# A batched matrix product: VectorE as a loop of four turns, and transfers that wait for VectorE's finished copies

## The chip, the cores and the metric

The kernel runs on one core of a Trainium2 chip. The time is the device time of one execution in microseconds (us); three runs of the kernel before gave 513.1, 514.22 and 514.61, median 514.22. The engines are called PE (TensorE), DVE (VectorE), ACT (ScalarE), POOL (GpSimd) and SP (SyncE). Transfers between HBM and SBUF go through 16 DMA engines; the queue q0 holds those that POOL issues, q1 those that SP issues.

## The reference

```
x:      (32, 512, 1024) float32
weight: (32, 1024, 768) float32
return np.matmul(x, weight).astype(np.float32)
```

Thirty-two independent products, each of a 512 x 1024 matrix with a 1024 x 768 matrix.

## The kernel before

The batches are taken two at a time: 16 pairs, k = 0 to 15, and pair k holds the batches 2k and 2k + 1. Every engine has its own stream of instructions, written out by hand, and the streams meet only at semaphores.

**Loads (POOL).** A load casts float32 from HBM to bfloat16 in SBUF. The weights have four slots, for four batches. Batches 0 to 3 and 30 and 31 are loaded one at a time (L101), those between by pairs in one transfer (L97), which needs the slots of the pair two before. The rows of x have two slots, for two pairs (L110); x of pair 0 comes by SP in float32 and is cast by DVE and ACT (L279). POOL issues in a fixed order: the first five loads at once, then for each k from 0 to 13 x of pair k + 2, from k = 2 on the store of pair k - 2 (L118), and the weights of pair k + 2. It stops at each wait, so a late wait also holds back what is written behind it. All these transfers share q0.

**What the loads wait for.** Weights wait for `s_mm`, which PE raises at the end of each half set of matmuls, four times a batch: when it has reached `mm_done(b)`, all matmuls of batch b are done. x waits for `s_pt`, which PE raises after each of the eight groups of transposes of a pair: the x of pair k - 2 is then read.

**Transposes and products (PE).** PE is a loop over the pairs. It takes `s_xr` (x has landed), transposes x in eight groups g into two PSUM tiles `pt` (L173), takes `s_wr` for each batch (the weights have landed, L177), and multiplies: for each batch four row tiles mt, each of 8 x 2 matmuls, one of 512 columns (L165) and one of 256 (L138). Two row tiles make a set p, so a batch has two sets, and a set fills three PSUM banks. The number of an output set is j = 2b + p.

**Copies (DVE and ACT).** DVE copies each group of transposes to SBUF (`spread`, L226, in the last pair L224). Of each set, DVE copies the bank shared by the two row tiles (L269, two copies, which raise `s_d`) and half of the third bank (L271, which raises `s_dp`); ACT copies the first bank (L258, `s_a`) and the other half of the third (L261, `s_ap`). PE waits for `s_c` (spreads), `s_a` and `s_d` before it overwrites a bank. In DVE's straight stream the order for pair k is: eight spreads, the last set of pair k - 1, then the first three sets of pair k. The last set of a pair is thus copied after the spreads of the next pair.

**Stores.** A pair's outputs are stored in one transfer by POOL, two pairs late (`HELD`), once `s_ap` and `s_dp` show them copied; the last pairs go by SP (L118 and L123). There are four slots of outputs; the first set of a pair waits until the slot's last store has landed (`slot_free`), on DVE and on ACT each.

Of the kernel before, what the change touches and what calls it, by code (L numbers as in the profile page):

```python
# [8 lines left out]
BF16 = mybir.dt.bfloat16  # L9
# [3 lines left out]
def kernel(  # L13
# [6 lines left out]
    nc = tc.nc  # L20
    B, M, K = x.shape
# [4 lines left out]
    KT = K // P  # L26
# [3 lines left out]
    PAIRS = B // 2  # L30
    HELD = 2
    GROUPS = 2 * MT
    W_SLOTS, X_SLOTS, OUT_SLOTS = 4, 2, 4

    pe, dve, act, pool, sp = nc.tensor, nc.vector, nc.scalar, nc.gpsimd, nc.sync
# [7 lines left out]
    def sbuf(name, shape, dtype):  # L43
        return nc.alloc_sbuf_tensor(name, shape, dtype).ap()
# [5 lines left out]
    both = [sbuf(f"xT{i}", [P, 2, JT, 2, H, 2], BF16) for i in range(MT)]  # L50
# [3 lines left out]
    pts = [nc.alloc_psum_tensor(f"pt{i}", [P, JT, P], F32).ap() for i in range(2)]  # L54
# [6 lines left out]
    def sem(name):  # L61
        sems.append(nc.alloc_semaphore(name))
        return sems[-1]
# [2 lines left out]
    s_w = [sem(f"s_w{i}") for i in range(W_SLOTS)]  # L66
    s_x = [sem(f"s_x{i}") for i in range(X_SLOTS)]
    s_wr, s_xr = sem("s_wr"), sem("s_xr")
    s_pt, s_c, s_mm = sem("s_pt"), sem("s_c"), sem("s_mm")
    s_a, s_ap, s_d, s_dp = sem("s_a"), sem("s_ap"), sem("s_d"), sem("s_dp")  # L70
    s_st = [sem(f"s_st{i}") for i in range(OUT_SLOTS)]
    s_fin = sem("s_fin")

    def mm_done(b):
        return 4 * (b + 1)

    def pt_done(k):
        return GROUPS * (k + 1)  # L80

    def last_out(b):

# [5 lines left out]
    def together(b):  # L89
        return W_SLOTS <= b < B - 2  # L90

    def load_w(b):
        if together(b):
            if b % 2 == 0:
                pool.wait_ge(s_mm, mm_done(b + 1 - W_SLOTS))
                slots = all_ws[:, b // 2 % 2].rearrange("p r ko n -> p r (ko n)")
                pool.dma_start(out=slots, in_=w_two_view[b // 2]).then_inc(s_w[b % W_SLOTS], 16)  # L97
            return
        if b >= W_SLOTS:
            pool.wait_ge(s_mm, mm_done(b - W_SLOTS))  # L100
        pool.dma_start(out=ws[b % W_SLOTS], in_=w_view[b]).then_inc(s_w[b % W_SLOTS], 16)  # L101

    def loads_of_w(b):
# [2 lines left out]

    def load_x(k):
        if k >= X_SLOTS:
            pool.wait_ge(s_pt, pt_done(k - X_SLOTS))
        pool.dma_start(out=xs[k % X_SLOTS], in_=x_view[k]).then_inc(s_x[k % X_SLOTS], 16)  # L110

    def copied(eng, j):
# [14 lines left out]
    def stationary(b, mt):  # L127
        return both[mt][:, b % 2].rearrange("p j h i r -> p j (h i) r")
# [7 lines left out]
    def other(out, weights, moving, first, last):  # L136

        return pe.add_instruction(  # L138
            mybir.InstMatmult(
                name=nc.get_next_instruction_name(),  # L140
                engine=mybir.EngineType.PE,
                ins=[pe.lower_ap(moving), pe.lower_ap(weights)],
                outs=[pe.lower_ap(out)],
                start_tensor_calc=first,
                stop_tensor_calc=last,
                tile_size=(P, P),
                tile_position=(0, 0),
                ldweights=False,
            )
        )  # L150

    def multiply(b, mt, w):
        pm, half = pms[mt // 2], mt % 2
        xT = stationary(b, mt)
        for ko in range(KT):
            for i, (bank, at, off, size) in enumerate(SPLITS[half]):
                args = (
                    pm[bank][:, at:at + size],
                    xT[:, ko // 2, :, ko % 2],
                    w[:, ko, off:off + size],  # L160
                )
                if i:
                    last = other(*args, ko == 0, ko == KT - 1)
                else:
                    last = pe.matmul(*args, start=(ko == 0), stop=(ko == KT - 1))  # L165
        last.then_inc(s_mm, 1)

    def transpose(k, g):

# [43 lines left out]

    def spread(k, g):

        pt = pts[g % 2].bitcast(BF16).rearrange("p j (b i r) -> p j b i r", b=2, r=2)
        if k == PAIRS - 1:

            for b in range(2):
                rows = both[g // 2][:, b].rearrange("p j h i r -> p j (h i r)")
                rows = rows.rearrange("p j (m r) -> p j m r", r=2)[:, :, g % 2::2, :]
                last = dve.tensor_copy(rows, pt[:, :, b])  # L224
            return last
        return dve.tensor_copy(both[g // 2][:, :, :, g % 2].rearrange("p b j i r -> p j b i r"), pt)  # L226

    def slot_free(eng, a):
        if a >= OUT_SLOTS:
            eng.wait_ge(s_st[a % OUT_SLOTS], 16 * (a // OUT_SLOTS))  # L230

    def columns(two_rows, i):

# [5 lines left out]
    def pieces(b, p, i):  # L239

        pm = pms[p][i]
        if i == 1:
            pm = pm.rearrange("p (t n) -> p t n", t=2)
        rows = [slice(0, H), slice(H, P)]
        at = p * N2
        if b >= B - 2:
            return [(columns(last_out(b)[half, at:at + N2], i), pm[half]) for half in rows]
        mine = outs[(b // 2) % OUT_SLOTS][H * (b % 2):H * (b % 2 + 1)]
        starts = [at + h * ROW for h in range(2)]
        return [(columns(mine[:, at:at + N2], i), pm[half]) for at, half in zip(starts, rows)]  # L250

    def out_on_act(b, p):
        j = 2 * b + p
        if b % 2 == 0 and p == 0:
            slot_free(act, b // 2)
        act.wait_ge(s_mm, 2 * j + 1)
        for piece in pieces(b, p, 0):
            last = act.copy(*piece)  # L258
        last.then_inc(s_a, 1)
        act.wait_ge(s_mm, 2 * j + 2)  # L260
        act.copy(*pieces(b, p, 2)[0]).then_inc(s_ap, 1)  # L261

    def out_on_dve(b, p):
        j = 2 * b + p
        if b % 2 == 0 and p == 0:
            slot_free(dve, b // 2)
        dve.wait_ge(s_mm, 2 * j + 2)
        for piece in pieces(b, p, 1):
            last = dve.tensor_copy(*piece)  # L269
        last.then_inc(s_d, 1)  # L270
        dve.tensor_copy(*pieces(b, p, 2)[1]).then_inc(s_dp, 1)  # L271

    def cast_first(eng, copy, rows):

        eng.wait_ge(s_first, 16)
        for mo in rows:
            if mo == 2 * MT - 1:
                eng.wait_ge(s_cast, 1)
            last = copy(xs[0][:, mo], x_first[:, mo])  # L279
        return last  # L280

    def on_dve():

        dve.sem_inc(s_d, 2)
        cast_first(dve, dve.tensor_copy, range(MT)).then_inc(s_cast, 1)
        for k in range(PAIRS):
            for g in range(GROUPS):
                dve.wait_ge(s_pt, GROUPS * k + g + 1)
                spread(k, g).then_inc(s_c, 1)
            for j in range(4 * k - 1, 4 * k + 3):  # L290
                if j >= 0:
                    out_on_dve(*divmod(j, 2))
        out_on_dve(B - 1, 1)

    def on_act():
        act.sem_inc(s_a, 2)
        cast_first(act, act.copy, range(MT, 2 * MT)).then_inc(s_xr, 1)
        for b in range(B):
            out_on_act(b, 0)
            if b % 2 and b < B - 1:  # L300
                landed(act, s_x[(b // 2 + 1) % X_SLOTS], (b // 2 + 2) // 2, s_xr)
            out_on_act(b, 1)
# [5 lines left out]
    def on_pool():  # L308
        load_w(0)
        pool.memset(ident, 0.0).then_inc(s_zero, 1)  # L310
        pool.wait_ge(s_zero, 1)
        pool.affine_select(  # L312
            out=ident,
            in_=ident,
            compare_op=mybir.AluOpType.not_equal,
            fill=1.0,
            base=0,
            pattern=[[-1, P]],
            channel_multiplier=1,
        ).then_inc(s_ident, 1)  # L320
        load_w(1)
        load_x(1)
        load_w(2)
        load_w(3)
        for k in range(PAIRS - 2):
            load_x(k + 2)
            if k >= 2:
                store(pool, k - 2, s_st[(k - 2) % OUT_SLOTS])
            load_w(2 * k + 4)
            load_w(2 * k + 5)  # L330
        for a in range(PAIRS - 2 - HELD, PAIRS - 2):
            store(pool, a, s_st[a % OUT_SLOTS])
# [21 lines left out]
    with tc.tile_critical(sync_engine=mybir.EngineType.Activation, no_gpsimd_drain=True):  # L354
        sp.dma_start(x_first, x_view[0]).then_inc(s_first, 16)
        on_pool()
        on_pe()
        on_dve()
        on_act()
        on_sp()  # L360
        clear_on_pool()
# [30 lines left out]
```

## Time and profile before

| what | value |
|---|---|
| median of three runs | 514.22 us |
| the profiled execution, its own time | 515.02 us |
| its span, first to last instruction | 512.9 us |
| PE busy | 430.9 us, 84% of the span |
| DVE busy | 212.9 us, 42%, 332 instructions |
| ACT busy | 116.4 us, 23% |
| POOL busy | 29.0 us, 6% |
| granted clock of PE, mean | 0.947 |
| stores on q0, issue to landing, median | 50.8 us |
| weights by pairs, issue to landing, median | 39.6 us |
| x, issue to landing, median | 43.2 us |

Busy times are those of one profiled execution, which ran 0.8 us longer than the median. A PE that is busy is not a PE at its peak, since the ends of matmuls are modelled. Waiting, branch and semaphore instructions don't count as busy. "Issue to landing" runs from the issuing instruction to the semaphore that says that all data is there, so it holds the time in the queue behind earlier transfers.

### The profile page before, as it was taken

To read this page: it belongs to the slowest core of one execution; us is meant where nothing else is said; L and a number is where in the kernel's file an instruction comes from. 1 tells how busy PE (TensorE), PEld (TensorE's weight loads), DVE (VectorE), ACT (ScalarE), POOL (GpSimd) and SP (SyncE) were. 2 spreads that over 40 slices of the span, in tenths; PEclk is the share of its full clock that TensorE was granted. 3 is DMA by queue.
4 is the path that set the end of the run, shared out by engine and by line. 5 is a ranking of instruction groups with operands and counts; after the bars stand their busy time and mean duration, and the time that the engine had idled before them with its cause. 6 is when DMAs were issued, how large, how long until landed. Compare 5 with 4: busy or idle time off the path is not lost. (4 is left out here: it accounts for less than half of the span.)

```text
span 512.9 us, 5613 instructions
## 1 busy us (share of the span) xinstructions
PE 430.9 (84%) x2512; PEld 174.7 (34%) x1536; DVE 212.9 (42%) x332; ACT 116.4 (23%) x197; POOL 29.0 (6%) x54
## 2 busy tenths in 40 slices
PE   0299999999997996969979699896997969989990
PEld 0143435353534242242423424224242332523420
DVE  0243736354545343352433524435353353533731
ACT  1313131313231221302213022130321303223130
POOL 2000001010101000010000100001000010000000
PEclk9999999999999998988989889899998989989996
DMA  8999999999999999999999999999999999999996
GB/s 293 263 212 215 221 222 206 226 293 246 219 338 214 335 222 229 323 219 339 217 245 308 219 336 216 272 287 219 333 218 290 265 220 339 216 299 254 366 427 253
DMA packets 9446, 136.37 MB, mean 266 GB/s; under 512 B 864, under 2 KB 864, under 8 KB 1376
## 3 DMA queue, kind: packets, MB, share of 16 engines
q0 software_dynamic: 8576, 125.83, 95.2%
q1 hardware_dynamic: 864, 10.49, 4.9%
q14 instruction: 6, 0.05, 0.0%
HBM read 167.77 MB, written 50.33 MB: 425 GB/s over the span
## 5 line engine op out<-in xcount | busy, mean ns | idle before, releaser
L165 PE MATMUL pm<-w,xT 128*128 x976 | 337.0, 394 | 0.0
L138 PE MATMUL pm<-w,xT 128*128 x1024 | 287.8, 281 | 36.2 <-PEq L177 29.0
L165 PEld LDWEIGHTS pm<-w,xT 128*128 128x128 bf16 x1024 | 103.4, 101 | 276.6 <-issue 275.9
L269 DVE COPY outs<-pm 64x512 f32<-64x512 f32 x128 | 88.1, 689 | 200.5 <-PE pm L138 199.1
L258 ACT COPY outs<-pm 64x512 f32<-64x512 f32 x128 | 74.2, 580 | 275.5 <-PE pm L138 274.8
L173 PE MATMUL pt<-ident,x 128*128 128x128 f32 x512 | 84.9, 309 | 33.3 <-PEq L177 23.0
L226 DVE COPY xT<-pt 128x1024 bf16<-128x1024 bf16 x120 | 77.7, 687 | 66.0 <-PE pt L173 65.9
L173 PEld LDWEIGHTS pt<-ident,x 128*128 128x128 f32 x512 | 71.6, 210 | 48.6 <-issue 26.4
L261 ACT COPY outs<-pm 64x512 f32<-64x512 f32 x64 | 37.0, 578 | 91.5 <-PE pm L138 91.5
L271 DVE COPY outs<-pm 64x512 f32<-64x512 f32 x64 | 43.9, 686 | 0.0
L97 POOL DMA_DIRECT2D w<-in_weight_dram x13 | 9.2, 704 | 298.6 <-PE pm L138 298.6
L110 POOL DMA_DIRECT2D x<-in_x_dram x15 | 8.3, 554 | 90.0 <-PE pt L173 90.0
L279 DVE CAST x<-outs 128x1024 bf16<-128x1024 f32 x4 | 2.5, 688 | 18.8 <-DMA outs<-in_x_dram 18.8
L118 POOL DMA_DIRECT2D out_dram<-outs x14 | 7.5, 537 | 8.0 <-DVE outs L271 7.7
L279 ACT CAST x<-outs 128x1024 bf16<-128x1024 f32 x4 | 3.9, 1042 | 16.5 <-DMA outs<-in_x_dram 16.5
L224 DVE COPY xT<-pt 128x512 bf16<-128x512 bf16 x16 | 5.7, 417 | 4.2 <-PE pt L173 4.2
L101 POOL DMA_DIRECT2D w<-in_weight_dram x6 | 3.4, 565 | 26.6 <-PE pm L138 25.3
L279 ACT ACT_TABLE_LOAD x1 | 1.3, 1283 | 1.0 <-ACTq L354 1.0
L312 POOL TENSOR_SCALAR_AFFINE_SELECT ident<-ident 128x128 f32<-128x128 f32 x1 | 0.3, 283 | 0.2 <-POOL ident L310 0.2
L310 POOL MEMSET ident<- 128x128 f32 x1 | 0.2, 223 | 0.0
L376 POOL MEMSET const-float32-0.0<- 128x1 f32 x1 | 0.1, 100 | 0.2 <-issue 0.2
L376 POOL MEMSET const-bfloat16-1.0<- 128x1 bf16 x1 | 0.1, 103 | 0.0
(2 smaller groups left out, 0.2 us busy)
## 6 DMA issues: line engine op xcount, KB each, us to landing
out_dram<-outs POOLq DMA_DIRECT2D x14, 3072.0 KB, 50.8
w<-in_weight_dram POOLq DMA_DIRECT2D x13, 3072.0 KB, 39.6
x<-in_x_dram POOLq DMA_DIRECT2D x15, 2048.0 KB, 43.2
w<-in_weight_dram POOLq DMA_DIRECT2D x6, 1536.0 KB, 40.0
outs<-in_x_dram SPq DMA_DIRECT2D x1, 4096.0 KB, 17.8
out_dram<-outs SPq DMA_DIRECT2D x1, 3072.0 KB, 18.4
out_dram<-outs SPq DMA_DIRECT2D x4, 768.0 KB, 12.2
```

Of the source, the lines that this page charges most:

```text
L97: pool.dma_start(out=slots, in_=w_two_view[b // 2]).then_inc(s_w[b % W_SLOTS], 16)
L110: pool.dma_start(out=xs[k % X_SLOTS], in_=x_view[k]).then_inc(s_x[k % X_SLOTS], 16)
L118: eng.dma_start(out=two_view[a], in_=outs[a % OUT_SLOTS]).then_inc(sem, 16)
L138: return pe.add_instruction(mybir.InstMatmult(name=nc.get_next_instruction_name(), engine=mybir.EngineType.PE, ins=[pe.lower_ap(moving), p ...
L165: last = pe.matmul(*args, start=(ko == 0), stop=(ko == KT - 1))
L173: last = pe.transpose(pts[g % 2][:, j, :], words[:, mo, j::JT], ident)
L226: return dve.tensor_copy(both[g // 2][:, :, :, g % 2].rearrange("p b j i r -> p j b i r"), pt)
L258: last = act.copy(*piece)
L261: act.copy(*pieces(b, p, 2)[0]).then_inc(s_ap, 1)
L269: last = dve.tensor_copy(*piece)
L271: dve.tensor_copy(*pieces(b, p, 2)[1]).then_inc(s_dp, 1)
L279: last = copy(xs[0][:, mo], x_first[:, mo])
```

## The change

DVE's stream of 16 pairs becomes a loop of four turns over four pairs. A register `turn` counts the turns; branches leave out the copy of a set before the first pair and choose other copies in the last one. Constants can't tell the turns apart, so the semaphores that DVE waits for are counted down: `s_set` (new) is raised by PE once for each finished set and taken by DVE, `s_free` (new) is raised by ACT when it has seen that a slot is free, and `s_pt` is lowered by 32 at the end of each turn. With `s_pt` and `s_mm` no longer counts over the whole run, the loads wait for `s_dp`, DVE's last copy of a set.

```diff
+    def out_done(b):
+        return 2 * (b + 1)
+
+    def out_before(k):
+        return 4 * k
...
     def load_w(b):
         if together(b):
             if b % 2 == 0:
-                pool.wait_ge(s_mm, mm_done(b + 1 - W_SLOTS))
+                pool.wait_ge(s_dp, out_done(b + 1 - W_SLOTS))
...
         if b >= W_SLOTS:
-            pool.wait_ge(s_mm, mm_done(b - W_SLOTS))
+            pool.wait_ge(s_dp, out_done(b - W_SLOTS))
...
     def load_x(k):
         if k >= X_SLOTS:
-            pool.wait_ge(s_pt, pt_done(k - X_SLOTS))
+            pool.wait_ge(s_dp, max(out_before(k - X_SLOTS), 1))
...
-                    last = pe.matmul(*args, start=(ko == 0), stop=(ko == KT - 1))
-        last.then_inc(s_mm, 1)
+                    full = pe.matmul(*args, start=(ko == 0), stop=(ko == KT - 1))
+        if half:
+            full.then_inc(s_mm, 1)
+        last.then_inc(s_set if half else s_mm, 1)
...
+    def slot_free(a):
         if a >= OUT_SLOTS:
-            eng.wait_ge(s_st[a % OUT_SLOTS], 16 * (a // OUT_SLOTS))
+            act.wait_ge(s_st[a % OUT_SLOTS], 16 * (a // OUT_SLOTS)).then_inc(s_free, 1)
...
+    def set_on_dve(b, p):
+        dve.wait_ge(s_set, 1).then_inc(s_set, -1)
         for piece in pieces(b, p, 1):
             last = dve.tensor_copy(*piece)
         last.then_inc(s_d, 1)
...
+        dve.sem_inc(s_free, OUT_SLOTS)
+        turns = PAIRS // OUT_SLOTS
+        def spreads(k, copy):
             for g in range(GROUPS):
                 dve.wait_ge(s_pt, GROUPS * k + g + 1)
-                spread(k, g).then_inc(s_c, 1)
-            for j in range(4 * k - 1, 4 * k + 3):
-                if j >= 0:
-                    out_on_dve(*divmod(j, 2))
-        out_on_dve(B - 1, 1)
+                copy(g).then_inc(s_c, 1)
+        def sets(b):
+            dve.wait_ge(s_free, 1).then_inc(s_free, -1)
+            set_on_dve(b, 0)
+            set_on_dve(b, 1)
+            set_on_dve(b + 1, 0)
+        with nc.Fori(0, turns, engines=[mybir.EngineType.DVE], hint_back_edge=True):
+            for k in range(OUT_SLOTS - 1):
+                spreads(k, spread)
+                if k:
+                    set_on_dve(2 * k - 1, 1)
+                else:
+                    with dve.If_ne(turn, 0):
+                        set_on_dve(2 * OUT_SLOTS - 1, 1)
+                sets(2 * k)
+            k = OUT_SLOTS - 1
+            with dve.If_ne(turn, turns - 1):
+                spreads(k, spread)
+            with dve.If_eq(turn, turns - 1):
+                spreads(k, spread_last)
+            set_on_dve(2 * k - 1, 1)
+            with dve.If_ne(turn, turns - 1):
+                sets(2 * k)
+            with dve.If_eq(turn, turns - 1):
+                sets(B - 2)
+            step = GROUPS * OUT_SLOTS
+            dve.wait_ge(s_pt, step).then_inc(s_pt, -step)
+            dve.reg_add(turn, turn, 1)
+        set_on_dve(B - 1, 1)
```

In the changed file, L98 and L102 are the weight loads of L97 and L101, L112 the x load of L110, and L274 and L276 the copies of L269 and L271.

## The prediction

> **What bounds the kernel now.** I read the queues first (columns: packets, MB, share of the time of 16 engines).
>
> ```profile
> q0 software_dynamic: 8576, 125.83, 95.2%
> q1 hardware_dynamic: 864, 10.49, 4.9%
> HBM read 167.77 MB, written 50.33 MB: 425 GB/s over the span
> ```
>
> The two queues together fill 100% of the span. PE, the busiest engine, has 84%. Next the stages: one from the time when the pairs take 26.5 us, one from the time when they take 31.5 us (length, then busy us of each engine; DMA share and GB/s last).
>
> ```profile
> 60.00:86.00 26.00, 25.02 (x155) 10.47 (x95) 12.86 (x20) 6.59 (x12) 1.80 (x3) 1.00 1.00 212
> 188.00:219.50 31.50, 26.73 (x159) 10.82 (x97) 13.10 (x20) 6.89 (x13) 1.76 (x3) 0.95 1.02 266
> ```
>
> The DMA share is 1.0 in both, and PE is idle for almost 5 us of the second. What PE waits for is in its waits (total, times, longest):
>
> ```profile
> PE pm L138 <- PEq L177: 29.0, 8, 4.4
> ```
>
> L177 is the wait for weights. It comes in most pairs from 160 us on, never between 30 and 160 us. So PE sets the pace at first, while the transfers queue up; then the queue does. Over the whole run the queue never pauses, so **any time in which it is empty is added to the end**. That decides this case.
>
> How full the queue is when POOL issues is read from POOL's timeline and, for each issue, from the time to landing (last column).
>
> ```profile
> 51.62 0.70 POOL L97 DMA_DIRECT2D w<-in_weight_dram  x1 [20.45 <-PE pm L138]
> 57.30 0.56 POOL L110 DMA_DIRECT2D x<-in_x_dram  x1 [4.97 <-PE pt L173]
> 78.10 0.70 POOL L97 DMA_DIRECT2D w<-in_weight_dram  x1 [20.25 <-PE pm L138]
> 83.78 0.56 POOL L110 DMA_DIRECT2D x<-in_x_dram  x1 [4.97 <-PE pt L173]
> 84.35 0.54 POOL L118 DMA_DIRECT2D out_dram<-outs  x1
> ```
>
> The answers for the windows 30:31 (x of pair 2, issued at 30.63), 51:52, 57:58 and 78:79, in this order:
>
> ```profile
> x<-in_x_dram POOLq DMA_DIRECT2D x1, 2048.0 KB, 31.1
> ```
> ```profile
> w<-in_weight_dram POOLq DMA_DIRECT2D x1, 3072.0 KB, 24.7
> ```
> ```profile
> x<-in_x_dram POOLq DMA_DIRECT2D x1, 2048.0 KB, 29.0
> ```
> ```profile
> w<-in_weight_dram POOLq DMA_DIRECT2D x1, 3072.0 KB, 22.7
> ```
>
> So x(2) lands at 61.7, w(4,5) at 76.3, x(3) at 86.3, w(6,7) at 100.8: one after another, a pair of weights in 14.6 us and an x in 10.0. By the trace's packets the engines go over from x(2) to w(4,5) between 60.8 and 61.5 (middle 61.1), and from x(3) to w(6,7) between 85.0 and 85.9 (middle 85.3). The issues at 51.62 and 78.10 thus come 9.5 and 7.2 us ahead of the queue's end. These are the two thinnest covers of the run. Store 0, issued at 84.35, lands 34.2 us later at 118.5; a store takes 7.2 us (x(4) lands at 111.3). From there a pair costs the queue 14.6 + 10.0 + 7.2 = 31.8 us against PE's 26.5, and the cover grows by some 5 us a pair. At 188 us weights land 40.5 us after their issue: 26 us queued ahead.
>
> **The change part by part.**
>
> *Weights wait for DVE's last copy (s_dp) and no longer for the last matmul (s_mm).* The last copy of a pair stands on DVE behind the eight spreads of the next pair, which wait for PE's transposes. DVE's timeline:
>
> ```profile
> 57.76 1.39 DVE L269 COPY outs<-pm 64x512 f32<-64x512 f32 x2
> 59.08 0.69 DVE L271 COPY outs<-pm 64x512 f32<-64x512 f32 x1
> ...
> 84.24 1.39 DVE L269 COPY outs<-pm 64x512 f32<-64x512 f32 x2
> 85.55 0.69 DVE L271 COPY outs<-pm 64x512 f32<-64x512 f32 x1
> ```
>
> The L271 copies that release w(4,5) and w(6,7) end at 59.08 + 0.69 = 59.8 and at 86.2. The issues move from 51.6 to 59.8 and from 78.1 to 86.3: **8.2 us later**, and the cover of 9.5 and 7.2 becomes 1.3 and -1.0 us.
>
> What this leaves empty depends on the time L from POOL's issue to the first packet, which no issue into an empty queue shows in mid-run. The rows that bound it: the first weight load, at the start of the run, and SP's load of x, issued at 0.93 with its first packet at 1.9 (another queue, L = 1.0).
>
> ```profile
> 1.49 0.67 POOL L101 DMA_DIRECT2D w<-in_weight_dram  x1 [1.04 <-ACTq L354]
> ```
> ```profile
> q0 software_dynamic: 16, 0.20, 92.6%
> ```
>
> The second is the window 6:7; 1:6 has no packet of q0. By the packets the first begins at 6.23, so L = 4.7, of which up to 1.2 may be the wait for a running packet of x (1.22 us each): 3.5 to 4.7. I take 3.5, from the same queue and operation, at its low end since a first use may be slower.
>
> - First hole: 59.8 + 3.5 = 63.3 against 61.1: 2.2 us.
> - Second hole: x(3) then ends at 85.3 + 2.2 = 87.5; w(6,7) begins at 86.3 + 3.5 = 89.8: 2.3 us.
> - Third issue, w(8,9): DVE's copies before it end at 112.9, so it begins by 116.4. Store 0 ends at about 117.3 + 4.5 = 121.8: no hole, nor later.
>
> Sum: 89.8 - 85.3 = **4.5 us**; in general 1.0 + L, so 2.0 (SP's row) to 5.7 us.
>
> The Trainium skill ("DMA: Bandwidth & Descriptors", Specifications) gives a first-byte latency of about 1 us for transfers that GpSimd issues; by it the loss would be estimated at 2.0 us, while the only row of that queue here has 4.7 with the wait named above.
>
> Does PE stop in the early part? w(4,5) lands at about 78.5 and is needed at 83.8; w(6,7) at about 105.3, needed at 110.4. No. The loss returns later: weights land 4.5 us later in every pair from 160 us on, the waits at L177 begin earlier and take the sum up. With 26 us queued ahead, an issue 8.2 us later leaves some 17 there: nothing more is lost per pair.
>
> *x waits for s_dp too.* Its issue moves from 57.3 to about 60.5, behind w in the same queue, as before, and the store after it by the same 3 us. Queue order on POOL is unchanged; w and x now go out in one burst. x(2) waits for the first copy (ends 37.8, was issued at 30.6); w(3) lands only at 52.1. Nothing. At the end, w(31) moves from 443.4 to 451.6, where the last L271 ends; it landed at 482.8 with 32 us ahead of its own 7.3, and PE needs it at about 490. Nothing.
>
> *The loop and branches on DVE.* DVE's instructions in the built program go from 356 to 168; the copies executed are the same. A back edge with branches is shown on PE: L173's idle by "issue" is 26.4 us in 16 pieces, 23.0 of it the first, so 0.23 us for each of the others. Four turns with some six branches each make about 6 us on DVE at that price, but most stand ahead of a spread, where DVE is idle for 3.7 us a pair, or ahead of a copy. The issues of w(4,5) and w(6,7) have no branch since the first turn's start ahead of them. Cost 0; uncovered, up to 0.2 us at the place of each hole.
>
> *s_set, s_free, and the earlier s_mm for half sets.* ACT's third copy may start one 256-wide matmul earlier (0.28 us); DVE is the last at the end, so nothing is gained. ACT reaches the wait for a slot ahead of DVE. Cost 0. Gain, at most those 0.28 us.
>
> **Time.** The profiled execution took 515.0 (span 512.9 and 2.1 around it): 519.5 after. It lies 0.8 above the median of 514.2, so I forecast **518.7** for the median.
>
> **Rivals.**
> - *Quick start of the queue*: L near 1.0 as in SP's row, a loss of 2.0, 516.2. For it: the 4.7 may hold first-use costs. Against: it is the only row of this queue. 0.13.
> - *Not slower: the hole is made up for.* If PE and not the queue sets the end, 4.5 us of hole are caught up and the time stays at 514.2; the point is whether the queue has 4.5 us to spare anywhere after 90 us. For it: the chain of waits of the last 93 us is all PE, and in 508:512 the queue is nearly idle. Against: the share of 1.02 in mid-run; PE's start in pair 14 (451.17) follows the landing of its weights (410.41 + 40.1 = 450.5), so PE's end hangs on the queue. 0.15; with the scatter of 513.1 to 514.6 this holds all chance of faster.
> - *Stalls on DVE*: each back edge or skipped block makes DVE wait for instructions. The instruction queue moves 6 packets in the span now. A stall decides only beyond DVE's 3.7 us of idle time plus the queue's cover, 5 us at the first edge (near 125 us) and 17 later; 10 us there would add about 1.5, to 520 or more. 0.07. The Trainium skill ("Runtime: NRT & Kernel Launch", Instruction fetch mechanics) says that a taken branch to a target outside two blocks of 256 instructions must fetch it first; no run here shows such a stall yet.
> - *The change doesn't do what it says* (issues not later): the waits in the diff leave no room. 0.
>
> **How the numbers follow.** Forecast 0.65 (517 to 520.5 by L and the scatter), the rivals as above. A measurement of this kernel tells 0.3% (1.5 us) from no change. Slower: 0.65 + 0.07 + most of 0.13 = 0.84; same: 0.11; faster: 0.05. The range runs from 514.8, which takes in the quick start, to 522, which takes in L = 4.7 and some of the stalls.
>
> **What would show it.** POOL's L98 issues at about 59.8 and 86.3 with landings of w(4,5) near 78.5 and w(6,7) near 105; a DMA share clearly under 1 near 62 and 88 and nowhere else; waits for weights that begin a pair earlier. The forecast is wrong if the share shows no hole, if holes show elsewhere (in late pairs above all), or if PE waits for DVE.

## The result and the profile after

| | before | changed |
|---|---|---|
| median of 6 runs each | 513.72 us | 517.25 us |
| ratio, 95% interval | | 1.007 (1.0051 to 1.0088) |
| profiled execution, own time | 515.02 us | 517.05 us |
| its span | 512.9 us | 515.3 us |

The changed kernel is slower by 3.5 us, with an interval of 2.6 to 4.5 us (0.51 and 0.88% of 513.7). 518.7 was forecast.

The queues of the changed kernel, in the same view as before:

```profile
q0 software_dynamic: 8576, 125.83, 95.1%
q1 hardware_dynamic: 864, 10.49, 4.9%
HBM read 167.77 MB, written 50.33 MB: 423 GB/s over the span
```

The bytes are the same, and the rate over the span fell from 425 to 423 GB/s. A hole of some 2 us doesn't show in a share of 515. It must be looked for in the stages. First POOL's timeline of the changed kernel, then the landings of the two weight loads in it (windows 59:60.3 and 86:86.8):

```profile
59.88 0.71 POOL L98 DMA_DIRECT2D w<-in_weight_dram  x1 [21.35 <-DVE outs L276]
60.57 0.56 POOL L112 DMA_DIRECT2D x<-in_x_dram  x1
86.36 0.71 POOL L98 DMA_DIRECT2D w<-in_weight_dram  x1 [25.23 <-DVE outs L276]
```
```profile
w<-in_weight_dram POOLq DMA_DIRECT2D x1, 3072.0 KB, 17.6
```
```profile
w<-in_weight_dram POOLq DMA_DIRECT2D x1, 3072.0 KB, 17.3
```

The issues come at 59.9 and 86.4, released by DVE's L276 and no longer by PE. The loads land 17.6 and 17.3 us later, where 24.7 and 22.7 were shown before. A load of this size takes 14.6 us when it follows another, so almost nothing was queued ahead any more. Its weights are there at 77.5 and 103.7, 1.2 and 2.9 us later than before.

Two stretches of 5 us, of the kernel before and of the changed one (length, busy us of PE, PEld, DVE, ACT, POOL, granted clock, DMA share, GB/s):

```profile
61.00:66.00 5.00, 4.95 (x32) 1.52 (x16) 1.98 (x3) 1.73 (x3) 0.00 (x0) 1.00 1.08 229
85.00:90.00 5.00, 5.00 (x33) 1.55 (x16) 2.36 (x4) 1.74 (x3) 0.00 (x0) 1.00 1.08 229
```
```profile
61.00:66.00 5.00, 4.95 (x32) 1.50 (x16) 1.98 (x3) 1.74 (x3) 0.13 (x1) 1.00 1.04 192
85.00:90.00 5.00, 5.00 (x32) 1.47 (x15) 2.25 (x4) 1.74 (x3) 1.79 (x3) 1.00 0.70 121
```

PE's 5.00 of 5.00 says that nothing is lost there at that moment. The queue moved 192 and 121 GB/s in place of 229, with a share of 0.70 in the second stretch. In the first the share stays at 1.04 though fewer bytes move: there the packets take longer, of which more below. The second hole shows alone in one microsecond, before and after:

```profile
86.00:87.00 1.00, 1.00 (x8) 0.32 (x4) 0.24 (x1) 0.72 (x2) 0.00 (x0) 1.00 0.98 209
```
```profile
86.00:87.00 1.00, 1.00 (x8) 0.29 (x3) 0.06 (x1) 0.90 (x2) 0.64 (x1) 1.00 0.02 0
```

PE gets the bill later, in its first wait for weights (window 160:180, before and after):

```profile
PE pm L138 <- PEq L177: 2.0, 1, 2.0
```
```profile
PE pm L140 <- PEq L182: 5.5, 1, 5.5
```

It grew by 3.5 us, some 75 us after the hole that caused it.

### The profile page after: what moved, and what is told of

The parts are those of the page before. It is cut to its first block, busy times and chain, and to the rows that moved or that the text cites. A ratio compares the mean times of both kernels' runs of the same rounds, so it can differ in the third digit from the quotient of the medians.

```text
span 515.3 us, 5719 instructions
## 1 busy us (share of the span) xinstructions
PE 429.7 (83%) x2512; PEld 174.5 (34%) x1536; DVE 212.9 (41%) x332; ACT 116.4 (23%) x197; POOL 28.9 (6%) x54
## 5 line engine op out<-in xcount | busy, mean ns | idle before, releaser
L140 PE MATMUL pm<-w,xT 128*128 x1024 | 287.4, 281 | 41.2 <-PEq L182 35.7
L274 DVE COPY outs<-pm 64x512 f32<-64x512 f32 x128 | 88.1, 689 | 206.1 <-DVEq L272 204.7
L224 DVE COPY xT<-pt 128x1024 bf16<-128x1024 bf16 x120 | 77.7, 687 | 64.4 <-PE pt L178 64.3
L269 ACT COPY outs<-pm 64x512 f32<-64x512 f32 x64 | 37.0, 578 | 85.3 <-PE pm L167 85.3
L276 DVE COPY outs<-pm 64x512 f32<-64x512 f32 x64 | 43.9, 687 | 0.0
L98 POOL DMA_DIRECT2D w<-in_weight_dram x13 | 9.2, 706 | 362.5 <-DVE outs L276 362.5
L112 POOL DMA_DIRECT2D x<-in_x_dram x15 | 8.3, 556 | 32.8 <-DVE outs L276 32.8
L102 POOL DMA_DIRECT2D w<-in_weight_dram x6 | 3.4, 566 | 29.9 <-DVE outs L276 28.7
```

The costliest lines, as they stand in the source:

```text
L140: return pe.add_instruction(mybir.InstMatmult(name=nc.get_next_instruction_name(), engine=mybir.EngineType.PE, ins=[pe.lower_ap(moving), p ...
```

## The experiments

The theory: two holes in the queue near 62 and 87 us, caused by the later issue of the weights, are the whole loss. The rivals: A, the loop with its branches and counted-down semaphores costs the time; B, each of the 14 late issues loses a little; C, the later x does. Ratios are against the kernel before on the same chip, with 95% intervals; its medians there were 514.23 (23 runs, first four experiments) and 514.32 (29 runs, last four).

**Weights on DVE's copies, without the loop.** The kernel before, with

```diff
-                pool.wait_ge(s_mm, mm_done(b + 1 - W_SLOTS))
+                pool.wait_ge(s_dp, out_done(b + 1 - W_SLOTS))
-            pool.wait_ge(s_mm, mm_done(b - W_SLOTS))
+            pool.wait_ge(s_dp, out_done(b - W_SLOTS))
```

> The kernel before, DVE's straight stream kept; only the weight loads wait for DVE's last copy (s_dp). Theory (two holes in the queue, near 62 and 87 us): +2.9 to +3.6 us against the kernel before, the DMA share near 0.4 to 0.6 in 61:62 and 86:87, weights of batches 6 and 7 landing near 103.7. Rival A (the loop, its branches and the counted-down semaphores cost the time): 0. Rival B (each of the 14 late issues loses about 0.25 us): +3.5, but with no hole.

Measured: 517.12, ratio 1.0053 (1.0037 to 1.007). The same two stretches of this run:

```profile
61.00:66.00 5.00, 4.95 (x32) 1.52 (x16) 1.98 (x3) 1.74 (x3) 0.30 (x1) 1.00 1.00 184
85.00:90.00 5.00, 5.00 (x33) 1.55 (x16) 2.35 (x4) 1.74 (x3) 1.79 (x3) 1.00 0.76 131
```

The rates are close to those of the changed kernel, and so is the loss within the intervals. The share missed the 0.4 to 0.6 expected in both places: in 86:87 it is 0.02 with no bytes moved, in 61:62 it reads 1.40 at 172 GB/s (234 before), and 0.34 in 62:63. Two lines of waits are enough to make it; rival A isn't needed.

**The loop, with early weights.** The changed kernel, with

```diff
-        if half:
-            full.then_inc(s_mm, 1)
-        last.then_inc(s_set if half else s_mm, 1)
+        last.then_inc(s_mm, 1)
...
-                pool.wait_ge(s_dp, out_done(b + 1 - W_SLOTS))
+                pool.wait_ge(s_mm, mm_done(b + 1 - W_SLOTS))
-            pool.wait_ge(s_dp, out_done(b - W_SLOTS))
+            pool.wait_ge(s_mm, mm_done(b - W_SLOTS))
...
-        act.wait_ge(s_mm, 2 * j + 2)
+        act.wait_ge(s_mm, 2 * j + 2).then_inc(s_set, 1)
```

> The changed kernel with its loop, branches and counted-down semaphores; only the weight loads wait for the last matmul (s_mm) again, and ACT hands s_set on to DVE. Theory of the holes: 0 against the kernel before (within 0.3%), no hole, although x still waits for s_dp. Rival A (the loop costs): +3.5. Rival C (the later x costs): +3.5.

Measured: 513.58, ratio 0.9989 (0.9977 to 1.0001). Its stretches:

```profile
61.00:66.00 5.00, 4.95 (x31) 1.47 (x15) 1.98 (x3) 1.74 (x3) 0.00 (x0) 1.00 1.06 224
85.00:90.00 5.00, 5.00 (x33) 1.47 (x15) 2.20 (x5) 1.74 (x3) 1.09 (x2) 1.00 1.10 233
```

The weights are issued at 51.16 and 77.64 again, and the rates are back. The edit also moves the raising of `s_set` from PE to ACT, so it returns more than the two waits; that these alone make the loss is what the kernel above shows. The loop and branches on DVE cost nothing that can be measured, nor does the later x that this kernel keeps. Rivals A and C fall.

**Only the two thin places, and all the others.** The kernel before, with the wait on `s_dp` for pairs 2 and 3 alone (`if b < 8`), and in a second kernel for all pairs but these (`if b >= 8`, and the single loads at the end).

> The kernel before; only the weight loads of pairs 2 and 3 wait for s_dp. Theory of the holes: the whole loss, +2.9 to +3.6 us. Rival B (a little in every pair): +0.5.

Measured: 517.2, ratio 1.0061 (1.0044 to 1.0078).

> The kernel before; all weight loads but those of pairs 0 to 3 wait for s_dp. Theory of the holes: 0 (within 0.3%), since 15 us and more are queued ahead there even with an issue 8 us later. Rival B (a little in every pair): +3.

Measured: 514.09, ratio 0.9998 (0.9984 to 1.0013). Two of the late issues make the whole loss and the others make none, though nearly all are as late. Rival B falls.

**Two other delays.** The kernel before, with the loads by pairs waiting for the next pair's transposes, and in a second kernel for one more set of DVE's copies:

```diff
-                pool.wait_ge(s_mm, mm_done(b + 1 - W_SLOTS))
+                pool.wait_ge(s_pt, pt_done(b // 2 - 1))
```
```diff
-                pool.wait_ge(s_mm, mm_done(b + 1 - W_SLOTS))
+                pool.wait_ge(s_dp, out_done(b + 1 - W_SLOTS) + 1)
```

> The kernel before; weight loads by pairs wait until the next pair's transposes are done (s_pt), so that they are issued near 57.3 and 83.8 us, 5.7 us later than before and 2.5 us earlier than in the changed kernel. With 1.5 us from issue to first packet, as the changed kernel shows it, the first load is in time by 2.3 us and the second just so: theory of the holes 0 to +0.5 us. If the start took the 3.5 us of the prediction: +2.0. Rival B (loss grows with the delay in every pair): +2.4.

Measured: 514.59, ratio 1.0006 (0.9996 to 1.0017). The issues came at 57.02 and 83.50. The +2.0 of a start of 3.5 us and the +2.4 of rival B both lie outside the interval. The second issue was still not quite in time:

```profile
85.00:90.00 5.00, 5.00 (x32) 1.56 (x16) 2.36 (x5) 1.74 (x3) 0.30 (x1) 1.00 0.96 179
```

By the trace's packets this issue comes 1.9 us ahead of the queue's end, its first packets take 1.13 us on average where 0.93 is usual, and the middle one of the 16 engines is 0.8 us later after w(6,7) than before, and 1.2 us from store 0 on. In the time this doesn't stand out.

> The kernel before; weight loads by pairs wait for one more set of DVE's copies, the first of the next pair, so that they are issued near 64.3 and 90.9 us, 4.5 us later than in the changed kernel. Theory of the holes: first packets near 65.8 and 92.4 against 85.3 of before, +7 to +8 us, the first hole now the larger one (about 4.7 us). Rival B (loss in proportion to the delay in every pair, 12.7 against 8.2 us): +5.4.

Measured: 524.49, ratio 1.0194 (1.018 to 1.0207), a loss of 10.2 us where 7 to 8 was expected. The issues came at 64.20 and 90.84. Its stretches where the holes are:

```profile
61.00:66.00 5.00, 4.95 (x32) 1.52 (x16) 1.98 (x3) 1.74 (x3) 1.25 (x2) 1.00 0.24 29
90.00:95.00 5.00, 4.95 (x32) 1.47 (x15) 1.78 (x3) 1.74 (x3) 1.79 (x3) 1.00 0.62 103
```

A share of 0.24 at 29 GB/s is the empty queue itself, while PE is busy for 4.95 of 5 us beside it. An issue 5.7 us late costs at most 0.9 us (the interval's end), one 8.2 us late 3.5, one 12.7 us late 10.2. That is no price per microsecond: the cost begins about where the cover ends (a cover of 4.1 us lost nothing, one of 1.9 us some 0.8 in the queue). By the trace's transfers this last kernel's queue runs 8.4 us behind that of before from 126 us on, most of it the two holes; then it loses 1.8 us more between 343 and 481 us. The packets there show where most of it goes: x's last packets ahead of a store take up to 2.3 us where 1.23 is usual (1.0 us more per engine than before, summed over this stretch), and the first packets of weights on a few engines up to 2.05 where 0.93 is usual (0.4 us more). Why is open. The issues of weights there come 3.2 to 4.6 us before the middle engine is through with what is queued; they land after 20.7 to 22.7 us, of which 14.6 is the load itself.

**The changed kernel, mended by another cut of the loads.** The first replaced loads go out batch by batch, each when its own slot is free:

```diff
     def together(b):
-        return W_SLOTS <= b < B - 2
+        return 2 * W_SLOTS <= b < B - 2
```

> The changed kernel; the weights of batches 4 to 7 are loaded one batch at a time, each when its own slot is free (near 43, 59.8, 69.4 and 86.3 us), so that batch 4 fills the queue past 68 and batch 6 past 90. All waits stay on s_dp. Theory of the holes: no hole, 0 against the kernel before (within 0.3%). Rivals A and C (loop, later x): +3.5.

Measured: 514.21, ratio 0.9996 (0.9986 to 1.0007). POOL's first two such issues:

```profile
42.89 0.53 POOL L102 DMA_DIRECT2D w<-in_weight_dram  x1 [4.66 <-DVE outs L276]
59.58 0.53 POOL L102 DMA_DIRECT2D w<-in_weight_dram  x1 [16.16 <-DVE outs L276]
```

The second of them is as late as in the changed kernel, but the first one has filled the queue past it. All waits still stand on `s_dp`. What costs is thus not the late wait but the queue that is empty behind it.

**x on DVE's copies.** The kernel before, with only the x loads waiting for `s_dp`.

> The kernel before; only the loads of x wait for s_dp as in the changed kernel. Theory of the holes: 0 (within 0.3%), since the weights issued at 51.6 and 78.1 us fill the queue until 75 and 100. Rival C (the later x costs): +3.5.

Measured: 514.53, ratio 1.0 (0.9986 to 1.0013). x is issued at 59.46 and 85.94, behind weights that are already queued: nothing is lost. No version here is faster than the kernel before by more than the intervals allow.

## Why the prediction was right, step by step

- *The queue bounds the kernel, and what it loses early isn't made up for.* Right. By the trace's transfers the queue of the changed kernel runs 1.0 us late after w(4,5), 3.3 after w(6,7), 3.8 after x(4) and 3.9 after store 0, and stays at 3.9 until 485 us (middle of the 16 engines). The rival that the hole is made up for falls.
- *Where the holes are.* Right: the two thin covers and nowhere else. The sign named for them holds for the second alone: near 62 the share falls under 1 only in 62:63 (0.75), and 61:62 reads 1.41; there the bytes show the hole.
- *The time from issue to first packet.* Mis-sized. 3.5 us was taken, from the first load of the run; measured by the trace's packets it is 1.5: 59.88 to 61.40 and 86.36 to 87.91 (middle of 16 engines) in the changed kernel, 64.20 to 65.78 and 90.84 to 92.35 in the kernel of the longest delay. The first load takes 4.6 to 4.7 us to the earliest packet in these same runs too, where the holes have 1.4 on that measure, so it was a poor stand-in: the row nearest in kind was not the nearest in state. The rival of a quick start, which had 0.13, was nearer in this term than the forecast. The 1 us of the Trainium skill ("DMA: Bandwidth & Descriptors", Specifications) was nearer than the row that I took.
- *A term that was missing: the restart.* The first packet of each engine after a hole takes 1.5 us on average over the 16, against 0.93 in the kernel before. That is 0.6 us per hole. With both numbers the sums come out within 0.2 us: the first hole 0.3 + 0.6 (1.0 measured), the second 87.9 - 86.35 + 0.6 = 2.2 (2.3 measured); for the longest delay 4.65 + 0.6 (5.3 measured) and 1.65 + 0.6 (2.4 measured).
- *The sum of 4.5 us.* Near by luck in part, since two errors run against each other. The formula with the right 1.5 gives 2.5, and as it goes by the start of w(6,7), it already holds the first hole and its restart. The second restart adds 0.6. Another 0.6 comes at x(4), just ahead of the first store: the last two packets of x on most engines take more than the usual 1.23 us in both kernels, on average 1.61 and 1.39 before, 1.47 and 2.13 after. Why is open. Together 3.7 against 3.9 by the transfers; the time itself moved by 3.5.
- *Which DMA engine ends the run.* Not in the prediction. The profiled execution moved by 2.0 only. The figures above are of the middle engine, but a landing, and the end of the run, wait for the slowest of the 16. It trails the middle one at the end of w(31) by 4.1 us in the profile before (482.5 against 478.4, landing at 482.8) and by 2.6 in the changed kernel's (484.8 against 482.2), so there it is 2.3 us late. In all ten profiled executions the span ends 30.4 to 30.5 us after that moment. The 0.07 in 508:512, which the prediction took for a queue nearly idle, is from 509.1 us on a single row of packets, back to back as of one engine, until 511.7. The lag differs between executions, from 2.0 to 4.4 us, so a sum against one execution has this scatter on top; what makes it is open.
- *Cost 0 for the loop, the branches, the later x and the late pairs.* Right, each by an experiment of its own. DVE's wait for transposes is 64.3 us in 62 pieces after and 65.9 in 62 before: no stall for instructions shows. The Trainium skill ("Runtime: NRT & Kernel Launch", Instruction fetch mechanics) has such a stall for branches that leave two blocks of 256 instructions; a program of 168 gave no case of it here.
- *Waits for weights begin a pair earlier.* Wrong: they begin at the same pair and are longer there, 5.5 against 2.0. Nor does the sum of these waits tell the loss: it is 35.7 us in the changed kernel and 35.9 in the one with early weights, which is some 4 us faster by the two ratios.

## What to carry to other kernels

When one transfer queue sets the time, ask of every wait that stands ahead of an issue how much is queued at that moment, not how late the wait is: here 8 us of delay cost the whole loss at two places and nothing that can be measured at all the others. The thinnest covers are here near the start: until the first store a pair costs the queue 14.6 + 10.0 = 24.6 us and PE 26.5, so the queue catches up with the issues, and only with the 7.2 us of a store does its cover grow. A hole can be closed without touching the wait, by cutting the load that stands ahead of it so that a part goes out when its own slot is free.

## What the hardware showed

- From POOL's issue into an empty queue to the first packet: 1.51 to 1.58 us at four holes in mid-run (middle of the 16 engines; 1.4 to the earliest), but 5.0 us for the first load of a run (4.6 to 4.7 to the earliest). Why the first takes three times as long isn't settled.
- The first packets after a hole take 1.5 us instead of 0.93, so a hole costs 0.6 us beyond its length, and a share of the time of packets reads above 1.0 in it (1.04 at 192 GB/s in 61:66): share and bytes must be read together.
- The 16 DMA engines of one queue don't stay together: by w(31), at some 480 us, the slowest is 2.0 to 4.4 us behind the middle one, and it sets the landings and the end of the run.
